# A two-layer diffusion trunk on one core: merge gates in a ring, the gated sums spread over all PSUM banks, and the modulation in other buffers

## The chip, the cores and the metric

One core of a Trainium2 chip runs the whole program in one launch. The metric is device time in microseconds (us), the median of the runs; lower is better. A profiled execution of the same kernel gives the rows that are read below.

## What is computed

The reference is one step of a two-layer trunk for 128 context tokens and 256 latent tokens (together T = 384 columns), with a model width of 1024. Cut to what matters here, a layer is

```python
mod   = silu(c) @ w_ada + b_ada                    # six vectors of 1024 for each of two token groups
h     = rmsnorm(x) * (1 + scale1) + shift1
y[n]  = branch n of h, 256 wide                    # retention, S5, gated linear, neighbourhood attention
merge = sum over n of sigmoid(h @ w_merge[n] + b_merge[n]) * (y[n] @ w_branch[n])
x     = x + gain1 * rmsnorm(merge @ w_out)
x     = x + gain2 * rmsnorm(relu(h2 @ w_mlp1)**2 @ w_mlp2)
```

All of it is in fp32. A product of two fp32 matrices is made of three matmuls of fp32r halves: high by high, low by high and high by low.

## The kernel before

Activations lie with the model width on the 128 partitions, as 8 tiles of 128 x 384, each as a high and a low half. Weights come as blocks of 128 x 1024 (512 KB) in one fixed order, written down in `weights`. The queue of the SP engine loads a block into `wf` (three buffers), the ScalarE engine (ACT) copies its high half to `wh`, the VectorE engine (DVE) subtracts to get the low half `wl` (three buffers each), and TensorE (PE) uses both. `gemm_a` multiplies one block with all 8 tiles: 24 matmuls into one PSUM bank. `next_w` hands out the next pair of halves, and moves each of the background jobs on by one piece. A job is a generator; `thin(job, 5, 4)` lets it move on in four of five such calls.

The compiler front end lays the instructions out by priority and by its own estimate of time, and puts a wait wherever an instruction needs a buffer that another still holds. On the chip every engine, and the SP queue, then takes its instructions in that fixed order. `first()` raises the priority of what is emitted under it; a job started with `PR_BG` is put 150 places back.

PSUM has eight banks, in three rings: `mm` (3), `mx` (3) and `my` (2).

The merge has 8 output tiles. For each, four gates (n = 0 to 3) are needed: `gates` makes them with four `gemm_a` into `mm`, and ACT takes each bank out with a tanh (L1415). `up` makes the four branch products of one output tile, 24 matmuls with the 6 of one branch in one bank of `mm`; DVE multiplies each bank with its gate (L1430) into `c1` (four buffers), GpSimd (POOL) adds two pairs (L1432, L1433), DVE adds the two sums (L1434), and `split` writes the high half with ACT (L121) and the low half with DVE (L122). `mixers` emits the branches' work and the first 16 gates, two rows of eight (`gt0` in `rC`, `gt1` in `rB`). `merge` then emits up 0, 1, eight gates, up 2, 3, eight gates, up 4, 5, 6, 7. After that `out_proj` loads x again (L1484, into `rX`, where the low halves of the branches were) and adds up rows of `w_out` in six banks (`acc`).

The modulation of a later part of the layer is worked out beside that. `silu_c` prepares two broadcast rows in `fa` and `fb`; for each of 24 blocks `ada` loads a block of `w_ada` (L602, into `r3`, two buffers) and runs two DVE products with a sum over the row (L604), each with its unused result in `mid` (three buffers). This job starts after the first four gates. `fb` also holds the queries, the output and the values of the neighbourhood attention, so `silu_c` cannot fill it before `put_branches` has split that output. `mid` serves the S5 output job too (`mk`, `w`, the GLU weights), and `r3` the retention job.

Of the kernel before, what the change touches and what calls it, by code (L numbers as in the profile page):

```python
# [15 lines left out]
AF = mybir.ActivationFunctionType  # L16
# [27 lines left out]
LAG0 = 2  # L44
ADA_MIX, ADA_MLP, S5_MLP = (5, 4), (2, 1), (4, 1)
NA_RATE = 2
# [8 lines left out]
class Kernel:  # L55
# [193 lines left out]
    def acc(self):  # L249

        b = [self.mmps(512), self.mmps(512), self.mmps(512), self.xps(), self.yps(), self.yps()]
        return b[0:2], b[2:4], b[4:6]

# [147 lines left out]
    def s5_setup(self):  # L401
# [6 lines left out]
        lre, lim, ldt = prm[:, 0], prm[:, 1], prm[:, 2]  # L408
        self.s5_x0 = prm[:, 3:5]
        dt, xr, xi, e = (self.sm(sh) for _ in range(4))  # L410
# [169 lines left out]
    def silu_c(self):  # L580

        nc = self.nc
        self.cb = [self.tile("fa", [128, D]), self.tile("fb", [128, 1536])[:, 0:D]]
        for g in range(2):
            cb, th = self.cb[g], self.mid([128, D])
            nc.sync.dma_start(cb, self.d["c2"][g:g + 1, :].to_broadcast([128, D]))
            nc.scalar.activation(th, cb, AF.Tanh, scale=0.5)
            nc.vector.scalar_tensor_tensor(cb, th, 1.0, cb, op0=ADD, op1=MUL)
# [6 lines left out]

    def ada(self, l, cm, first, count):

        nc = self.nc
        cols, mod = cm
        for n in range(first, first + count):  # L600
            w = self.r3([128, D])
            nc.sync.dma_start(w, self.d["w_ada"][l, n])  # L602
            for g in range(2):
                nc.vector.scalar_tensor_tensor(self.mid([128, D]), w, 0.5, self.cb[g], op0=MUL, op1=MUL,  # L604
                                               accum_out=mod[:, n, g:g + 1])
            yield
        fs = slice(first, first + count)
        b = cols[:, C_BADA + first:C_BADA + first + count].unsqueeze(2).to_broadcast([128, count, 2])
        nc.vector.tensor_tensor(mod[:, fs], mod[:, fs], b, op=ADD)
# [12 lines left out]
    def ada_first(self, xt):  # L622
# [4 lines left out]
        self.cols, self.mod = cols, mod = self.cm[0]  # L627
        fb = self.tile("fb", [128, 1536])
        cs, sel = fb[:, 0:256].rearrange("p (k m) -> p k m", k=8), fb[:, 256:260]
# [11 lines left out]
        for t in range(1, KT):  # L641
            if t == 2:
                self.s5prm = self.load("s5prm", "s5_prm", [128, 5, 16 * DEPTH], eng=nc.sync)
                with self.background(PR_SET):
                    self.s5_setup()
            if t == RAW4:
                raw = self.mid([128, 1024])
                nc.sync.dma_start(raw, self.stream.pop(0))
                self.raws.append(raw)
            ws.append(self.ada_load(t))  # L650
# [237 lines left out]
    def head_norm(self, o, gate, gn):  # L888
# [3 lines left out]
        for i in range(2):  # L892
# [5 lines left out]
            for j in range(3):  # L898
                nc.tensor.matmul(vps[:, i * 6 + 2 * j:i * 6 + 2 * j + 2], sq[:, j * 128:(j + 1) * 128], self.bones,
                                 start=True, stop=True)  # L900
        r = self.few(12)
        nc.vector.tensor_scalar(r, vps[:, 0:12], EPS, None, op0=ADD)
# [430 lines left out]
    def na_in(self, l, hs, first):  # L1333
        nc = self.nc
        self.ft = self.row("rE", shape=(128, 3072))
        self.nk = self.tile("fa", [128, 2, 512])
        fb = self.tile("fb", [128, 1536])
        self.nq = fb[:, 0:768].rearrange("p (a n) -> p a n", a=2)
        self.nv = fb[:, 768:1536].rearrange("p (a n) -> p a n", a=3)
        nc.gpsimd.dma_start(self.nk[:, :, T:512], self.d["na_k"][l])  # L1340
# [62 lines left out]

    def gates(self, tag, j, hs, within=None):

        nc = self.nc
        gt = self.row(tag)
        for e in range(2):
            if e and within:
                within()  # L1410
            for n in range(4):
                ps = self.mmps()
                self.gemm_a(ps, hs)
                c = n * 8 + 2 * j + e
                nc.scalar.activation(gt[:, e * 4 + n], ps, AF.Tanh, scale=0.5, bias=self.bmrg_h[:, c:c + 1])  # L1415
        return gt

    def up(self, dt, gt, mgh, mgl):

        nc = self.nc  # L1420
        wh, wl = self.next_w(jobs=False)
        us = []
        for n in range(4):
            ps = self.mmps()
            for k in range(2):
                ws = slice((2 * n + k) * 128, (2 * n + k + 1) * 128)
                self.mm3(ps, wh[:, ws], wl[:, ws], self.brh[:, 2 * n + k], self.brl[:, 2 * n + k], k == 0, k == 1)
            u = self.c1()
            with self.first():
                nc.vector.scalar_tensor_tensor(u, gt[:, (dt % 2) * 4 + n], 1.0, ps, op0=ADD, op1=MUL)  # L1430
            us.append(u)
        nc.gpsimd.tensor_tensor(us[0], us[0], us[1], op=ADD)  # L1432
        nc.gpsimd.tensor_tensor(us[2], us[2], us[3], op=ADD)  # L1433
        nc.vector.tensor_tensor(us[0], us[0], us[2], op=ADD)  # L1434
        self.split(mgh[:, dt], mgl[:, dt], us[0])

    def mixers(self, l, hs, hook, first):
# [18 lines left out]
        s5 = self.start(self.s5_out(l))  # L1456
        gt0 = self.gates("rC", 0, hs, lambda: hook("gates"))
        self.finish(s5)
        gt1 = self.gates("rB", 1, hs)
        self.finish(gla, ret)  # L1460
        self.put_branches()
        return gt0, gt1

    def merge(self, hs, gt0, gt1):

        mgh, mgl = self.row("rA", F32R), self.row("rD", F32R)
        self.up(0, gt0, mgh, mgl)
        self.up(1, gt0, mgh, mgl)
        gt2 = self.gates("rC", 2, hs)
        self.up(2, gt1, mgh, mgl)  # L1470
        self.up(3, gt1, mgh, mgl)
        gt3 = self.gates("rB", 3, hs)
        self.up(4, gt2, mgh, mgl)
        self.up(5, gt2, mgh, mgl)
        self.up(6, gt3, mgh, mgl)
        self.up(7, gt3, mgh, mgl)
        return [(mgh[:, k], mgl[:, k]) for k in range(KT)]
# [59 lines left out]
    def layer(self, l, hs, hook, first):  # L1537
# [6 lines left out]
        if l:  # L1544
            for i in range(3):
                nc.gpsimd.dma_start(d["x_mid"][i], self.x[:, i])
        gt0, gt1 = self.mixers(l, hs, hook, first)
        mg = self.merge(hs, gt0, gt1)
        hs, first = self.out_proj(l, mg)
# [8 lines left out]
    def weights(self, l):  # L1558
# [4 lines left out]
        br = [d["w_branch"][l, i] for i in range(8)]  # L1563
        out += mrg[0:16] + br[0:2] + mrg[16:24] + br[2:4] + mrg[24:32] + br[4:8]
        out += [d["w_out"][l, i] for i in range(8)]
# [7 lines left out]
    def run(self):  # L1573
# [11 lines left out]
        for l in range(DEPTH):  # L1585

            def hook(where):
# [7 lines left out]
                if where == "gates":  # L1595
                    self.silu_c()
                    job = chain(self.ada(l, cm[l], 16, 8), self.ada(l, cm[l], 24, 16))
                    self.start(self.thin(job, *ADA_MIX), 1, PR_BG)
                if where == "norm3" and l == 0:
                    job = chain(self.ada(0, cm[0], 40, 8), self.ada(1, cm[1], 0, 16))  # L1600
                    self.start(self.thin(job, *ADA_MLP), 1, PR_BG)
# [3 lines left out]
                if where == "norm3" and l:  # L1605
                    self.start(self.thin(self.ada(l, cm[l], 40, 8), *ADA_MLP), 1, PR_BG)

# [192 lines left out]
```

## Time and profile before

| | us |
|---|---|
| median of 3 runs | 1474.38 |
| the runs | 1471.38 to 1475.14 |
| the profiled execution, its own time | 1479.85 |
| its span, first to last instruction | 1478.1 |
| PE busy in the span | 1404.9 |
| DVE busy in the span | 933.3 |

The profiled execution is 5.5 us (0.4%) above the median. Busy time of PE counts matmuls that overlap each other, so the idle time of PE and the rate at which matmuls start say more than its busy share. In layer 0 the branches' last work and the first 16 gates run from about 222 to 320 us, the merge from 320 to 440 us and the output projection's rows after it; in layer 1 the merge runs from 1039 to 1158 us. The profile has 24 `w_ada` blocks in each layer's part of this.

### The profile page before, as it was taken

How to read it: one execution, taken by the hardware profiler on the slowest of the kernel's cores; microseconds unless marked ns; L12 is line 12 of the kernel's file. 1: busy time of each engine (PE TensorE's matmuls, PEld its weight loads, DVE VectorE, ACT ScalarE, POOL GpSimd, SP SyncE). 2: the span in 40 equal slices, each digit the busy share in tenths (PEclk: the TensorE clock that was granted, in tenths of full speed). 3: DMA queues.
4: the chain of work that ended last, by engine and by line, in shares of the span. 5: the costliest groups of instructions: out<-in, count | busy, mean ns of one | idle time of the engine just before them, and what ended most of it. 6: DMA issues, size and time to landing. Idle time of an engine off the chain costs nothing. (4 is left out here: it accounts for less than half of the span.)

```text
span 1478.1 us, 22360 instructions
## 1 busy us (share of the span) xinstructions
PE 1404.9 (95%) x8492; PEld 1246.4 (84%) x8492; DVE 933.3 (63%) x1480; ACT 664.7 (45%) x1235; POOL 352.8 (24%) x654
## 2 busy tenths in 40 slices
PE   6989989988998999999999999999799999999998
PEld 5868868878996888888989888689799789999896
DVE  4497952799565767776363397359974658333334
ACT  3446454523335544444464646544233355444443
POOL 5973790011120213320011691000110200000000
PEclk9999999999999999999999999999899999999999
DMA  9546323576434465666446423146663527433342
GB/s 379 156 128 209 113 93 101 169 236 228 134 120 166 164 197 186 198 225 199 153 139 204 142 94 111 51 154 220 210 192 125 195 73 227 135 129 126 128 152 86
DMA packets 93629, 238.17 MB, mean 161 GB/s; under 512 B 17969, under 2 KB 39505, under 8 KB 93521
## 3 DMA queue, kind: packets, MB, share of 16 engines
q1 hardware_dynamic: 90656, 227.75, 47.2%
q0 software_dynamic: 2864, 8.98, 1.9%
q8 instruction: 67, 1.10, 0.3%
q14 instruction: 42, 0.34, 0.1%
HBM read 221.72 MB, written 14.97 MB: 160 GB/s over the span
## 5 line engine op out<-in xcount | busy, mean ns | idle before, releaser
L155 DVE TENSOR_TENSOR wl<-wf,wh 128x1024 fp32r<-128x1024 f32 (+1 forms) x254 | 320.3, 1263 | 294.0 <-ACT wh L143 291.7
L143 ACT CAST wh<-wf 128x1024 fp32r<-128x1024 f32 (+1 forms) x254 | 264.5, 1045 | 453.4 <-PE mm L209 169.7
L208 PE MATMUL mm<-hh,wh 128*128 128x384 f32 (+1 forms) x712 | 246.4, 346 | 5.4 <-DVE c L1430 4.1
L210 PE MATMUL mm<-hh,wl 128*128 128x384 f32 (+1 forms) x712 | 245.0, 344 | 0.0
L209 PE MATMUL mm<-hl,wh 128*128 128x384 f32 (+1 forms) x712 | 244.4, 343 | 0.0
L208 PE MATMUL mx<-hh,wh 128*128 128x384 f32 x448 | 151.1, 337 | 0.0
L210 PE MATMUL mx<-hh,wl 128*128 128x384 f32 x448 | 150.5, 336 | 0.0
L209 PE MATMUL mx<-hl,wh 128*128 128x384 f32 x448 | 150.4, 336 | 0.0
L208 PEld LDWEIGHTS mm<-hh,wh 128*128 128x128 f32 (+1 forms) x712 | 134.6, 189 | 12.1 <-DVE c L1430 4.1
L209 PEld LDWEIGHTS mm<-hl,wh 128*128 128x128 f32 (+1 forms) x712 | 134.7, 189 | 6.3 <-issue 4.2
L210 PEld LDWEIGHTS mm<-hh,wl 128*128 128x128 f32 (+1 forms) x712 | 134.5, 189 | 5.9 <-issue 4.0
L604 DVE SCALAR_TENSOR_TENSOR mid<-r,fa 128x1024 f32<-128x1024 f32 x80 | 101.1, 1264 | 30.7 <-DMA r<-w_ada 20.5
L604 DVE SCALAR_TENSOR_TENSOR mid<-r,fb 128x1024 f32<-128x1024 f32 x80 | 100.2, 1253 | 0.2
L209 PE MATMUL mm<-wl,rA 128*128 128x512 f32 x216 | 86.8, 402 | 0.0
L208 PEld LDWEIGHTS mx<-hh,wh 128*128 128x128 f32 x448 | 84.2, 188 | 2.8 <-issue 1.0
L209 PEld LDWEIGHTS mx<-hl,wh 128*128 128x128 f32 x448 | 84.2, 188 | 1.8
L210 PEld LDWEIGHTS mx<-hh,wl 128*128 128x128 f32 x448 | 84.2, 188 | 0.2
L208 PE MATMUL mm<-wh,rA 128*128 128x512 f32 x216 | 80.2, 403 | 0.7 <-ACT rA L121 0.7
L210 PE MATMUL mm<-wh,rB 128*128 128x512 f32 x180 | 70.3, 392 | 0.0
L706 POOL TENSOR_TENSOR few<-few,negh 128x1 f32<-128x1 f32 x24 | 13.3, 553 | 220.5 <-DVE few L705 213.6
L721 POOL DMA_DIRECT2D gain<-g x4 | 2.2, 553 | 245.8 <-ACT g L720 245.8
L121 ACT CAST rA<-c 128x384 fp32r<-128x384 f32 x80 | 41.0, 513 | 44.1 <-DVE c L1434 42.3
(523 smaller groups left out, 2984.6 us busy)
## 6 DMA issues: line engine op xcount, KB each, us to landing
wf<-w_mlp SPq DMA_DIRECT2D x128, 512.0 KB, 3.4
r<-w_ada SPq DMA_DIRECT2D x82, 512.0 KB, 3.9
wf<-w_merge SPq DMA_DIRECT2D x64, 512.0 KB, 3.4
wf<-w_in SPq DMA_DIRECT2D x43, 512.0 KB, 3.9
wf<-w_branch SPq DMA_DIRECT2D x16, 512.0 KB, 3.8
wf<-w_out SPq DMA_DIRECT2D x16, 512.0 KB, 3.3
s_vt<-mid SPq DMA_DIRECT2D x16, 256.0 KB, 3.0
mid<-s_vt SPq DMA_DIRECT2D x8, 512.0 KB, 4.6
```

The lines of the kernel that those rows point to most:

```text
L121: self.nc.scalar.copy(hi, src)
L143: self.nc.scalar.copy(wh[:, :cols], raw)
L155: self.nc.vector.tensor_tensor(wl[:, :cols], raw, wh[:, :cols].bitcast(F32), op=SUB)
L208: mm(out, lh, rh, start=start, stop=False)
L209: mm(out, lh, rl, start=False, stop=False)
L210: mm(out, ll, rh, start=False, stop=stop)
L604: nc.vector.scalar_tensor_tensor(self.mid([128, D]), w, 0.5, self.cb[g], op0=MUL, op1=MUL, accum_out=mod[:, n, g:g + 1])
L706: self.nc.gpsimd.tensor_tensor(r, v, self.negh[:, 0:1], op=ALU.pow)
L721: nc.gpsimd.dma_start(d[l, which].rearrange("g (k f) -> (g k) f", f=128), rows)
```

## The change

It does four things.

- `merge` emits up(t) and then the four gates of tile t + 4, for t = 0 to 3, and then up 4 to 7. A gate tile goes to the place in `rC` or `rB` that up(t) has just read, so the two rows are a ring of four tiles. The `w_branch` blocks are moved to match in `weights`.
- `up` takes its four banks from all three rings: `my`, `my`, `mm`, `mx` for an even tile and `mx`, `mx`, `mm`, `mm` for an odd one. `acc` asks for the same six banks in another order.
- `ada` gets its buffer as an argument: within the gates and the merge the `w_ada` blocks go to `mid`, in the later part to `r3` as before. The second product writes over the block itself, and only the first uses another `mid`.
- `fb` is split into `fq` (queries and output of the attention) and `fv` (its values). `silu_c` uses `fa` and `fv`. The job starts before the first gate, and at three pieces of four calls. To make room, the S5 parameters lie in `rs`, with a small copy `s5x0` made on POOL, and a small tile of `head_norm` moves from `few` to `sm`.

```diff
-ADA_MIX, ADA_MLP, S5_MLP = (5, 4), (2, 1), (4, 1)
+ADA_MIX, ADA_MLP, S5_MLP = (4, 3), (2, 1), (4, 1)
...
     def acc(self):
-        b = [self.mmps(512), self.mmps(512), self.mmps(512), self.xps(), self.yps(), self.yps()]
-        return b[0:2], b[2:4], b[4:6]
+        b = [[self.yps(), self.yps()], [self.mmps(512), self.xps()], [self.mmps(512), self.mmps(512)]]
+        return b[::-1]
...
-        self.s5_x0 = prm[:, 3:5]
+        self.s5_x0 = self.tile("s5x0", [128, 2, n])
+        v.tensor_copy(self.s5_x0, prm[:, 3:5])
...
-        self.cb = [self.tile("fa", [128, D]), self.tile("fb", [128, 1536])[:, 0:D]]
+        self.cb = [self.tile("fa", [128, D]), self.tile("fv", [128, D])]
...
-    def ada(self, l, cm, first, count):
+    def ada(self, l, cm, first, count, buf):
...
-            w = self.r3([128, D])
+            w = buf([128, D])
             nc.sync.dma_start(w, self.d["w_ada"][l, n])
             for g in range(2):
-                nc.vector.scalar_tensor_tensor(self.mid([128, D]), w, 0.5, self.cb[g], op0=MUL, op1=MUL,
+                nc.vector.scalar_tensor_tensor(w if g else self.mid([128, D]), w, 0.5, self.cb[g], op0=MUL, op1=MUL,
                                                accum_out=mod[:, n, g:g + 1])
...
-        fb = self.tile("fb", [128, 1536])
-        self.nq = fb[:, 0:768].rearrange("p (a n) -> p a n", a=2)
-        self.nv = fb[:, 768:1536].rearrange("p (a n) -> p a n", a=3)
+        self.nq = self.tile("fq", [128, 768]).rearrange("p (a n) -> p a n", a=2)
+        self.nv = self.tile("fv", [128, D])[:, 0:768].rearrange("p (a n) -> p a n", a=3)
...
+    def gates(self, gt, t, hs):
+
+        nc = self.nc
+        for n in range(4):
+            ps = self.mmps()
+            self.gemm_a(ps, hs)
+            c = n * 8 + t
+            nc.scalar.activation(self.gate(gt, t)[:, n], ps, AF.Tanh, scale=0.5, bias=self.bmrg_h[:, c:c + 1])
+
+    def gate(self, gt, t):
+        return gt[t // 2 % 2][:, t % 2 * 4:t % 2 * 4 + 4]
...
+        banks = (self.xps, self.xps, self.mmps, self.mmps) if dt % 2 else (self.yps, self.yps, self.mmps, self.xps)
         for n in range(4):
-            ps = self.mmps()
+            ps = banks[n]()[:, 0:T]
...
-                nc.vector.scalar_tensor_tensor(u, gt[:, (dt % 2) * 4 + n], 1.0, ps, op0=ADD, op1=MUL)
+                nc.vector.scalar_tensor_tensor(u, self.gate(gt, dt)[:, n], 1.0, ps, op0=ADD, op1=MUL)
...
-        gt0 = self.gates("rC", 0, hs, lambda: hook("gates"))
+        gt = [self.row("rC")]
+        hook("gates")
+        self.gates(gt, 0, hs)
+        self.gates(gt, 1, hs)
         self.finish(s5)
-        gt1 = self.gates("rB", 1, hs)
+        gt.append(self.row("rB"))
+        self.gates(gt, 2, hs)
+        self.gates(gt, 3, hs)
...
-        self.up(0, gt0, mgh, mgl)
-        self.up(1, gt0, mgh, mgl)
-        gt2 = self.gates("rC", 2, hs)
-        self.up(2, gt1, mgh, mgl)
-        self.up(3, gt1, mgh, mgl)
-        gt3 = self.gates("rB", 3, hs)
-        self.up(4, gt2, mgh, mgl)
-        self.up(5, gt2, mgh, mgl)
-        self.up(6, gt3, mgh, mgl)
-        self.up(7, gt3, mgh, mgl)
+        for t in range(KT):
+            self.up(t, gt, mgh, mgl)
+            if t + 4 < KT:
+                self.gates(gt, t + 4, hs)
...
-        out += mrg[0:16] + br[0:2] + mrg[16:24] + br[2:4] + mrg[24:32] + br[4:8]
+        out += mrg[0:16]
+        for t in range(4):
+            out += [br[t]] + mrg[16 + 4 * t:20 + 4 * t]
+        out += br[4:8]
...
-                    job = chain(self.ada(l, cm[l], 16, 8), self.ada(l, cm[l], 24, 16))
+                    job = chain(self.ada(l, cm[l], 16, 8, self.mid), self.ada(l, cm[l], 24, 16, self.mid))
```

## Rows read from the trace of the kernel before

**Rows 1.** Waits of PE, whole span: for whom, total us, times, longest.

```profile
PE mm L208 <- DVE c L1430: 17.0, 12, 4.4
...
PE mm L208 <- ACT rC L143: 6.4, 2, 3.7
...
PE mm L209 <- DVE rX L122: 1.4, 2, 0.8
```

**Rows 2.** Windows: length, then busy us (instructions) of PE, PEld, DVE, ACT, POOL; granted clock, DMA share, GB/s.

```profile
222.00:281.00 59.00, 59.00 (x374) 50.56 (x371) 27.35 (x46) 26.69 (x55) 4.01 (x4) 1.00 0.43 123
281.00:320.00 39.00, 39.00 (x227) 35.53 (x227) 35.81 (x60) 15.58 (x25) 2.29 (x1) 1.00 0.67 216
320.00:372.00 52.00, 41.85 (x221) 39.21 (x220) 51.71 (x80) 14.32 (x21) 6.69 (x5) 0.93 0.68 223
372.00:418.00 46.00, 45.79 (x265) 45.47 (x264) 21.61 (x26) 16.70 (x22) 4.91 (x4) 1.00 0.40 129
...
1039.00:1090.00 51.00, 43.35 (x220) 41.63 (x219) 50.49 (x77) 13.99 (x19) 6.64 (x5) 0.90 0.70 225
```

**Rows 3.** The same windows, DVE's instructions of line 604 alone (read-outs counted too).

```profile
281.00:320.00 39.00, 24.09 (x41) 1.00 0.67 216
320.00:372.00 52.00, 35.42 (x56) 0.93 0.68 223
```

**Rows 4.** PE's timeline, layer 0: start, us, what; in brackets idle before, and for whom.

```profile
320.44 0.61 PE L208 MATMUL mm<-rE,wh 128*128 128x384 f32 x2
...
330.29 0.69 PE L208 MATMUL mm<-rE,wh 128*128 128x384 f32 x1 [4.42 <-DVE c L1430]
...
429.10 0.61 PE L208 MATMUL my<-wh,rA 128*128 128x512 f32 x2
...
439.52 0.39 PE L208 MATMUL mm<-wh,rA 128*128 128x512 f32 x1
440.21 0.40 PE L208 MATMUL mm<-wh,rA 128*128 128x512 f32 x1
```

**Rows 5.** PE's timeline, layer 1: the merge's first matmul and the first after it.

```profile
1039.39 0.34 PE L208 MATMUL mm<-rE,wh 128*128 128x384 f32 x1
...
1157.92 0.39 PE L208 MATMUL mm<-wh,rA 128*128 128x512 f32 x1
```

**Rows 6.** DVE's timeline in the merge of layer 0.

```profile
325.11 1.22 DVE L604 SCALAR_TENSOR_TENSOR mid<-r,fb 128x1024 f32<-128x1024 f32 x1
...
329.68 1.48 DVE L1430 SCALAR_TENSOR_TENSOR c<-rC,mm 128x384 f32<-128x384 f32 x3
...
341.89 2.03 DVE L604 SCALAR_TENSOR_TENSOR mid<-r,fa 128x1024 f32<-128x1024 f32 x1
...
350.63 1.21 DVE L155 TENSOR_TENSOR wl<-wf,wh 128x1024 fp32r<-128x1024 f32 x1
...
352.92 0.55 DVE L1434 TENSOR_TENSOR c<-c,c 128x384 f32<-128x384 f32 x1
```

**Rows 7.** Timelines of ACT and of the SP queue: the preparation for the modulation, layer 0.

```profile
247.12 1.06 ACT L587 ACTIVATE mid<-fa 128x1024 f32<-128x1024 f32 x1 [4.12 <-PE my L1016]
...
271.12 0.33 SPq L586 DMA_DIRECT2D fb<-c  x1
```

**Rows 8.** Timelines of SP, ACT and PE after the merge, layer 0.

```profile
439.54 1.87 SPq L1484 DMA_DIRECT2D rX<-x  x3
...
452.00 1.04 ACT L143 CAST rC<-wf 128x1024 fp32r<-128x1024 f32 x1 [6.57 <-DMA wf<-w_out]
...
455.38 0.63 PE L208 MATMUL mm<-rC,rA 128*128 128x512 f32 x1
...
456.66 0.63 PE L208 MATMUL mm<-wh,rA 128*128 128x512 f32 x1
```

**Rows 9.** Waits of the SP queue: for whom, total us, times, longest.

```profile
SPq L602 <- DVE mid L604: 146.6, 65, 4.1
SPq L1007 <- PE my L1020: 40.4, 2, 22.2
```

More of the change, by code (lines that the diff above doesn't have):

```diff
@@ L627, in ada_first @@
         self.cols, self.mod = cols, mod = self.cm[0]
-        fb = self.tile("fb", [128, 1536])
+        fb = self.tile("fv", [128, D])
         cs, sel = fb[:, 0:256].rearrange("p (k m) -> p k m", k=8), fb[:, 256:260]
@@ L642, in ada_first @@
             if t == 2:
-                self.s5prm = self.load("s5prm", "s5_prm", [128, 5, 16 * DEPTH], eng=nc.sync)
+                self.s5prm = self.tile("rs", [128, 768])[:, 0:80 * DEPTH].rearrange("p (a n) -> p a n", a=5)
+                nc.sync.dma_start(self.s5prm, self.d["s5_prm"])
                 with self.background(PR_SET):
@@ L900, in head_norm @@
                                  start=True, stop=True)
-        r = self.few(12)
+        r = self.sm([128, 12])
         nc.vector.tensor_scalar(r, vps[:, 0:12], EPS, None, op0=ADD)
@@ L1336, in na_in @@
         self.nk = self.tile("fa", [128, 2, 512])
-        fb = self.tile("fb", [128, 1536])
-        self.nq = fb[:, 0:768].rearrange("p (a n) -> p a n", a=2)
-        self.nv = fb[:, 768:1536].rearrange("p (a n) -> p a n", a=3)
+        self.nq = self.tile("fq", [128, 768]).rearrange("p (a n) -> p a n", a=2)
+        self.nv = self.tile("fv", [128, D])[:, 0:768].rearrange("p (a n) -> p a n", a=3)
         nc.gpsimd.dma_start(self.nk[:, :, T:512], self.d["na_k"][l])
@@ L1401, in na_mix @@
         self.out[3] = q
-    def gates(self, tag, j, hs, within=None):
+    def gates(self, gt, t, hs):
         nc = self.nc
[L1407 to L1411, printed above, removed]
-                ps = self.mmps()
[L1413 to L1416, printed above, removed]
+        for n in range(4):
[5 more added lines that the diff above has]
+        return gt[t // 2 % 2][:, t % 2 * 4:t % 2 * 4 + 4]
     def up(self, dt, gt, mgh, mgl):
@@ L1422, in up @@
         us = []
+        banks = (self.xps, self.xps, self.mmps, self.mmps) if dt % 2 else (self.yps, self.yps, self.mmps, self.xps)
         for n in range(4):
-            ps = self.mmps()
+            ps = banks[n]()[:, 0:T]
             for k in range(2):
@@ L1456, in mixers, with merge @@
         s5 = self.start(self.s5_out(l))
-        gt0 = self.gates("rC", 0, hs, lambda: hook("gates"))
+        gt = [self.row("rC")]
+        hook("gates")
+        self.gates(gt, 0, hs)
+        self.gates(gt, 1, hs)
         self.finish(s5)
-        gt1 = self.gates("rB", 1, hs)
+        gt.append(self.row("rB"))
+        self.gates(gt, 2, hs)
+        self.gates(gt, 3, hs)
         self.finish(gla, ret)
         self.put_branches()
-        return gt0, gt1
-    def merge(self, hs, gt0, gt1):
+        return gt
+    def merge(self, hs, gt):
         mgh, mgl = self.row("rA", F32R), self.row("rD", F32R)
-        self.up(0, gt0, mgh, mgl)
-        self.up(1, gt0, mgh, mgl)
-        gt2 = self.gates("rC", 2, hs)
-        self.up(2, gt1, mgh, mgl)
-        self.up(3, gt1, mgh, mgl)
-        gt3 = self.gates("rB", 3, hs)
-        self.up(4, gt2, mgh, mgl)
-        self.up(5, gt2, mgh, mgl)
-        self.up(6, gt3, mgh, mgl)
-        self.up(7, gt3, mgh, mgl)
+        for t in range(KT):
+            self.up(t, gt, mgh, mgl)
+            if t + 4 < KT:
+                self.gates(gt, t + 4, hs)
         return [(mgh[:, k], mgl[:, k]) for k in range(KT)]
@@ L1546, in layer @@
                 nc.gpsimd.dma_start(d["x_mid"][i], self.x[:, i])
-        gt0, gt1 = self.mixers(l, hs, hook, first)
-        mg = self.merge(hs, gt0, gt1)
+        gt = self.mixers(l, hs, hook, first)
+        mg = self.merge(hs, gt)
         hs, first = self.out_proj(l, mg)
@@ L1596, in hook @@
                     self.silu_c()
-                    job = chain(self.ada(l, cm[l], 16, 8), self.ada(l, cm[l], 24, 16))
+                    job = chain(self.ada(l, cm[l], 16, 8, self.mid), self.ada(l, cm[l], 24, 16, self.mid))
                     self.start(self.thin(job, *ADA_MIX), 1, PR_BG)
                 if where == "norm3" and l == 0:
-                    job = chain(self.ada(0, cm[0], 40, 8), self.ada(1, cm[1], 0, 16))
+                    job = chain(self.ada(0, cm[0], 40, 8, self.r3), self.ada(1, cm[1], 0, 16, self.r3))
                     self.start(self.thin(job, *ADA_MLP), 1, PR_BG)
@@ L1605, in hook @@
                 if where == "norm3" and l:
-                    self.start(self.thin(self.ada(l, cm[l], 40, 8), *ADA_MLP), 1, PR_BG)
+                    self.start(self.thin(self.ada(l, cm[l], 40, 8, self.r3), *ADA_MLP), 1, PR_BG)
             hs, first = self.layer(l, hs, hook, first)
```

## The prediction

> **What bounds the kernel now.** I read the waits of PE first: the engine with the most work should have few, and each has a name. Two names are near the change: PE waiting for the gated sums' DVE product, 12 times and 17.0 us, and for a weight cast at the end of the merge, 6.4 us [rows 1]. Then the windows by stage. While the first 16 gates run (222 to 320 us) PE is busy all the time; in the merge's first 52 us it is busy 41.9, at a granted clock of 0.93, and in the 46 us after that it loses 0.2 [rows 2]. Its count shows the size better: 265 matmuls in those 46 us are 0.174 us each, 221 in the 52 us are not enough to fill 39. In the bad window DVE has no room: 51.7 of 52 us, of which 35.4 are the modulation's products; in the next it works 21.6 of 46 [rows 2, 3]. Layer 1 has the same two neighbours [rows 2]. Last the timelines, for the order inside. At 320.4 PE starts the first gated sum; it stops for 4.42 us before 330.29, as the first three banks are emptied only at 329.7, behind a queue of modulation products on DVE [rows 4, 6]. So the local bound is DVE, and the three `mm` banks are how its delay reaches PE.
>
> **What the merge loses.** It holds 8 sums and 16 gates, 24 groups of 24 matmuls. At 0.174 us that is 100.0 us. Between the last sums PE also puts rows of the output projection, first at 429.10; its timeline has six such row halves before 439.52, three products each, and 18 products at 0.23 us (three between 439.52 and 440.21) are 4.2 us. So 104.2 us of work; it took 439.5 - 320.4 = 119.1 us, and 118.5 in layer 1 [rows 4, 5]. Lost: 14.9 and 14.3, **29.2 us** in both, the idle time and the slow clock after it together.
>
> **The change, part by part.**
>
> Ring order. Nothing is added: 24 groups of 24 in both. After each of the first four sums PE has four gates, 16.7 us, in which DVE can end that sum. A gate's tanh now waits for the product that reads its old place, and behind it on ACT wait the weight casts, and so PE. The first tanh falls due one gate (4.2 us) after the sum's last matmul, and its product some 3 us before that; so about 7 us of slack against a queue on DVE of at most 4.6 us now (325.1 to 329.7) [rows 6]. I cost it at nothing; without the cover it would be one cast and one gate, some 4 us, each of 8 times.
>
> DVE's load. A round of one sum and four gates is 20.9 us of PE. DVE has four products of about 0.5 (three take 1.48), the added pair and the low half of about 0.55 each, five weight halves of 1.21, and three blocks of modulation at 2 x 1.22: 2.0 + 1.1 + 6.1 + 7.3 = 16.5 us [rows 6]. Where POOL's two additions run beside it a DVE product takes 2.03 instead of 1.22 [rows 6]; two of those make 18.1. So DVE stays under PE, at 87%, where now it is at 99%.
>
> Where the modulation goes. Now it cannot start before `fb` is loaded, at 271.1, since the attention's output lies there; all 24 blocks (97 rows with the read-outs) then fall between 281 and 372 [rows 3, 7]. With `fv` that wait is gone, and the next in line is `mid`: the S5 output job holds it, and the preparation, which needs one, runs at 247.1 as soon as PE is done with it [rows 7]. I expect the first block at about 250. With three pieces in four calls, 16 calls give 12 blocks among the first gates and 16 more give 12 in the merge. In the gates' time DVE has 27.4 + 35.8 - 24.1 = 39.1 us of other work in 98; with 12 blocks, 29 us, it is at 70% [rows 2, 3]. That it is denser after 250 than before does no harm by the trace: between 281 and 320 it was 35.8 of 39, and PE lost nothing [rows 2].
>
> The banks. Eight instead of three for the sums let PE run two whole sums ahead of DVE. At the end four sums follow each other, 16.7 us of PE, against some 4.3 to 5.1 us of DVE each (four products, pair, low half, one weight half, and POOL's share): DVE falls back 1 to 4 us, which the banks hold. I cost this at nothing, or 1 us a layer where the last two banks are late for the row sums.
>
> What stays. PE's wait for the last branch's low half, 1.4 us in layer 0 [rows 1], is there whatever the order, as that branch ends with the last gates. So 29.2 - 1.4 = 27.8; I take **27**.
>
> The end of the merge. Loading x waits for the last sum, as it goes where the branches' low halves were: it is issued at 439.5, right after PE's last use. The next `w_out` blocks are issued behind it on SP, and the first is cast at 452.0, after a wait of 6.6 us; PE stood still for 3.7 us, and 2.7 in layer 1, and then ran four groups of three products at half the clock (1.28 us from 455.38 to 456.66, against 0.69 before), 2.3 us more [rows 1, 4, 8]. When the sums no longer wait for banks, the row products between them (4.2 us) come after them, so the loads are issued 4.2 us earlier against PE's work, more than the wait. At most that gives 3.7 + 2.7 + 2 x 2.3 = 11.0 us, at least nothing (if the scheduler still mixes rows in, or the row banks come late). The order of the banks speaks for the upper half, as a row bank is free only after the sixth sum: I take **7**.
>
> Small things. One copy of 64 columns on POOL in the setup, far from the end, and the in-place write: no further DVE or DMA work. S5's parameters, the small tile and the attention's two tiles change addresses only. Nothing taken, 1 us either way.
>
> **Sum.** 27 + 7 = 34 us. Against the profiled execution: 1479.9 - 34 = 1445.9. That execution is 5.5 us above the median, and none of the rows used says where, so I put the same saving on the median: 1474.4 - 34 = **1440**.
>
> **A rule beside it.** The rows say that the banks alone would not cure it, as DVE, which empties them, has 0.3 us left in 52 [rows 2]. The Trainium skill says otherwise, on its page "Perfetto Trace Analysis", section "Optimization Strategy": a gap that repeats on the engine that should be full can mean that PSUM has too few tiles. By that rule the 29 us come back even where the modulation stays bunched; by the rows only about half would. The change does both things, so the sum is the same, and only the first rival hangs on it.
>
> **The rivals.**
>
> *The modulation stays bunched.* It starts late, as `mid` is held until 247 and each block takes two of its three buffers, so that most of it still falls into the merge. For: the holder of `mid` [rows 7]. Against: 98 us of gates have room for 12 blocks [rows 2]. Then eight banks save about half of the merge's loss and little at the end: 1474 - 15 = 1459, between 1450 and 1464.
>
> *The load queue stands (slower).* SP takes its DMAs in order. Today it stands for 22.2 and 18.2 us before the S5 job's second load into `mid` [rows 9], and PE loses nothing, since six weight blocks are ahead, 6 x 4.2 = 25 us. Now `w_ada` blocks use `mid` too, and an issue that waits for it has the gates' weights behind it. The point from which it decides is a stand of 25 us; to eat up the 34 us it would take 17 us more in each layer, so 42 us. At 50 us it costs 25 in each layer, 1474 - 34 + 50 = 1490. For: twice the users of one ring. Against: the longest wait of a `w_ada` issue for its buffer's reader is 4.1 us in 65 [rows 9], and these loads have the lower priority. The Trainium skill, on its page "DMA: Bandwidth & Descriptors", section "Anatomy of one DMA — SWDGE (gpsimd) path", states that a DMA's semaphore wait happens on the issuing sequencer before dispatch; that is the same mechanism, and the trace agrees, with the 22.2 us.
>
> *The gain does not arrive.* What PE waits for in the merge is taken by another wait of the same size, of the tanh for its ring place or of a weight half behind modulation products. For: DVE at 87%. Against: the 7 us of slack. Time: within 4 us of 1474.
>
> **How the numbers follow.** The forecast has 0.58, with 1431 to 1449 (all of both terms, 1474.4 - 29.2 - 11 - 3 for the spread of the runs, to four fifths of the first alone, with 2 for the small things). The first rival has 0.26, the gain that does not arrive 0.09, the slower one 0.07. A measurement of this kernel tells about 0.3%, 4.4 us, from no change: faster is 0.58 + 0.26 = 0.84, same 0.09, slower 0.07. The range takes in the forecast and most of the first rival: 1431 to 1462.
>
> **What would show it.** PE's waits for the gated sums' product fall from 17 us to under 4; the merge takes about 100 us plus the row products, at full clock; the modulation's products begin near 250 and end near 405 in layer 0, and no window of DVE is full; x is loaded right after the last sum and PE's wait for the `w_out` cast is under 2 us. It is wrong if DVE is still full for 30 us from the merge's start, if PE waits for weights among the first gates, or if the row sums wait for their banks.

## The result, and the profile after

The kernel with the change takes 1455.87 us (1453.53 to 1458.91, 4 runs) where the kernel before takes 1473.93 beside it: ratio 0.9881, 95% interval 0.9854 to 0.9908, so 18 us faster. The forecast was 1440 and the range 1431 to 1462: the sign and the range held, but the saving is about half of the 34 us that the sum gave. Its profiled execution has a span of 1451.8 us against 1478.1. The boundary is the step behind a merge's row sums, with the residual and the next norm; PE's first product behind it (L291) marks the same work in both kernels, and so does PE's first product of layer 1. Cut at these marks, the spans compare as follows (us; "again" is a second profiled execution of each kernel, on other chips).

| stretch | before | after | before, again | after, again |
|---|---|---|---|---|
| start to the boundary of layer 0 | 478.8 | 460.8 | 481.9 | 464.9 |
| from there to layer 1's input | 291.0 | 292.3 | 291.0 | 291.6 |
| layer 1's input to its boundary | 426.2 | 416.2 | 422.7 | 417.8 |
| from there to the end | 282.1 | 282.5 | 282.1 | 282.5 |
| of these: first gated sum to boundary, layer 0 | 158.4 | 143.1 | 158.9 | 144.3 |
| first gated sum to boundary, layer 1 | 156.6 | 144.6 | 155.5 | 144.9 |
| layer 1's input to its first gated sum | 269.6 | 271.6 | 267.2 | 272.9 |

So the merges with their ends give back 27.3 us in the first pair and 25.2 in the second, and layer 1 ahead of its merge loses 2.0 and 5.7 of it again. Layer 0 ahead of its first gated sum is 2.7 and 2.5 shorter.

PE's waits after, whole span (for whom, total us, times, longest):

```profile
PE mx L901 <- DVE g L899: 4.5, 1, 4.5
PE mm L208 <- ACT rC L143: 4.2, 2, 2.3
PE mx L533 <- DVE c L574: 4.0, 1, 4.0
...
PE mx L208 <- ACT wh L143: 2.6, 2, 1.6
```

The 17.0 us for the gated sums' product [rows 1] are gone from the list altogether. A new wait of 4.5 us stands near the top: PE waits in layer 1 for a DVE copy of `head_norm` (L899). The wait of 4.0 us (L574) lies at 103 us, in the early part of layer 0; the kernel before has 0.8 there. The windows of the merges after, same columns as [rows 2], and below them DVE's modulation products alone (L605 now), as in [rows 3]:

```profile
320.00:372.00 52.00, 51.01 (x290) 50.21 (x290) 50.85 (x75) 18.94 (x25) 9.57 (x6) 1.00 0.66 214
372.00:418.00 46.00, 46.00 (x266) 46.00 (x265) 27.43 (x38) 16.77 (x22) 8.14 (x7) 1.00 0.41 137
1025.00:1077.00 52.00, 50.40 (x288) 49.86 (x287) 50.40 (x77) 17.32 (x23) 6.03 (x5) 1.00 0.67 221
```

```profile
250.00:281.00 31.00, 10.86 (x17) 1.00 0.70 216
281.00:320.00 39.00, 21.37 (x37) 1.00 0.66 207
320.00:372.00 52.00, 27.09 (x43) 1.00 0.66 214
```

In its first 52 us the merge now runs 290 matmuls at full granted clock, where 221 ran at 0.93 [rows 2]. The modulation did move forward: 10.86 us of it lie ahead of 281 us, none did before, and 27.09 instead of 35.42 fall into the merge. But DVE is still nearly full there, 50.85 of 52 (the prediction's round had it at 87%), and PE hardly notices. The end of the merge, SP, ACT and PE after:

```profile
420.04 1.37 SPq L1483 DMA_DIRECT2D rX<-x  x3
425.75 0.33 SPq L164 DMA_DIRECT2D wf<-w_out  x1
...
436.08 1.04 ACT L143 CAST rC<-wf 128x1024 fp32r<-128x1024 f32 x1 [4.39 <-DMA wf<-w_out]
...
437.18 0.51 PE L208 MATMUL mm<-rC,rA 128*128 128x512 f32 x1 [2.28 <-ACT rC L143]
```

x is loaded right behind the last sum, 19.5 us earlier than in [rows 8]; the late cast of `w_out` still stops PE for 2.28 us (3.7 before).

### The profile page after: what moved, and what is told of

The parts are those of the page before. It is cut to its first block, busy times and chain, and to the rows that moved or that the text cites. A ratio compares the mean times of both kernels' runs of the same rounds, so it can differ in the third digit from the quotient of the medians.

```text
span 1451.8 us, 22299 instructions
## 1 busy us (share of the span) xinstructions
PE 1394.5 (96%) x8492; PEld 1241.7 (86%) x8492; DVE 934.8 (64%) x1480; ACT 663.5 (46%) x1235; POOL 350.7 (24%) x655
## 5 line engine op out<-in xcount | busy, mean ns | idle before, releaser
L143 ACT CAST wh<-wf 128x1024 fp32r<-128x1024 f32 (+1 forms) x254 | 264.6, 1045 | 415.6 <-PE mx L209 170.8
L605 DVE SCALAR_TENSOR_TENSOR mid<-mid,fa 128x1024 f32<-128x1024 f32 x48 | 60.4, 1259 | 27.0 <-DMA mid<-w_ada 26.8
L605 DVE SCALAR_TENSOR_TENSOR mid<-mid,fv 128x1024 f32<-128x1024 f32 x48 | 60.0, 1250 | 0.2
L1432 POOL TENSOR_TENSOR c<-c,c 128x384 f32<-128x384 f32 x16 | 17.5, 1091 | 174.6 <-DVE c L1430 111.2
```

The lines of the kernel that those rows point to most:

```text
L143: self.nc.scalar.copy(wh[:, :cols], raw)
L605: nc.vector.scalar_tensor_tensor(w if g else self.mid([128, D]), w, 0.5, self.cb[g], op0=MUL, op1=MUL, accum_out=mod[:, n, g:g + 1])
```

## The experiments

### The parts one by one

The change has three parts: the **ring** (order of sums, gates and their weights), the **banks** (the sums' PSUM banks and the order of the row banks), and the **modulation** (buffers `fv`, `fq`, `mid`, and the start ahead of the gates). All combinations ran. The table gives the median, its ratio to the kernel before on the same chip, and PE's longest kinds of wait in the merges. In every run that has it, the modulation part includes its early start.

| run | ring | banks | modulation | us | ratio, 95% interval | PE waits in the merges (both layers) |
|---|---|---|---|---|---|---|
| e1 | - | - | - | 1478.46 | 1.0007, 0.9982 to 1.0031 | product 15.6 |
| e2 | - | - | yes | 1480.45 | 1.0008, 0.9981 to 1.0036 | product 8.2, last branch's split 7.3 |
| e4 | - | yes | - | 1476.80 | 0.9981, 0.9958 to 1.0005 | product 21.2 |
| e9 | yes | - | - | 1468.47 | 0.9911, 0.9878 to 0.9944 | product 12.6 |
| e3 | yes | yes | - | 1448.05 | 0.9790, 0.9761 to 0.9818 | none for either |
| e6 | yes | - | yes | 1480.74 | 1.0025, 1.0010 to 1.0039 | split 9.9, product 7.2 |
| e7 | - | yes | yes | 1478.77 | 1.0019, 1.0000 to 1.0039 | product 16.1 |
| e5 | yes | yes | yes | 1458.12 | 0.9876, 0.9854 to 0.9897 | product 0.4 |

Where the time goes in the profiles (us, from PE's timelines, cut as above):

| run | first gated sum to boundary, layer 0 and 1 | layer 1's input to its first gated sum |
|---|---|---|
| e1 (none) | 158.9, 155.5 | 267.2 |
| e2 (modulation) | 152.7, 151.6 | 280.2 |
| e4 (banks) | 159.1, 155.9 | 264.6 |
| e9 (ring) | 156.9, 148.3 | 267.4 |
| e3 (ring, banks) | 143.1, 146.1 | 264.2 |
| e6 (ring, modulation) | 150.6, 149.6 | 282.3 |
| e7 (banks, modulation) | 154.4, 155.0 | 273.4 |
| e5 (all) | 144.3, 144.9 | 272.9 |

In layer 1 of e3 and e4, 22 products of a gate (some 3.8 us) run behind the first gated sum that stand ahead of it in the others. In e2 and e6 the wait for the last branch's split comes just ahead of the first gated sum (4.6 and 7.0 us in layer 1), so it counts in the last column.

**e1, the kernel before again**, no edit.

> The kernel before, unchanged, profiled once more. If its first profiled execution was simply a slow one, the new span lies near 1472 us, and the merges (first gated sum to the load of x) take some 113 to 117 us each instead of 119.1 and 118.6. If a profile always shows it slow, the span is again 1477 to 1480 with merges of 118 to 120. The median stays within 0.3% of 1474.

1478.46 us, and its profile has merges of 119.6 and 117.7 us from first sum to the load of x, against 119.1 and 118.6: the profiled execution that the prediction read was typical of the merges.

**e2, the modulation alone.** The kernel before with its new buffers, three pieces in four, and the start ahead of the gates:

```diff
-        gt0 = self.gates("rC", 0, hs, lambda: hook("gates"))
+        hook("gates")
+        gt0 = self.gates("rC", 0, hs)
```

> The modulation's part alone (fv, fq, mid for the blocks, start before the first gate, three in four); the order of sums and gates and the three banks stay as before. If DVE's bunched modulation is the cause, most of the gain is here: 1460 to 1465, PE's waits for the gated sums' product fall from 17 to under 8 us, and DVE in the merge's first 52 us from 51.7 to about 40. If the banks are the cause, 1469 to 1474 with these waits still over 10 us.

```profile
320.00:372.00 52.00, 46.49 (x245) 45.26 (x246) 46.38 (x72) 15.81 (x23) 6.70 (x5) 0.93 0.62 200
```

```profile
PE mm L208 <- DVE c L1431: 8.2, 8, 2.8
PE mm L208 <- ACT rE L121: 7.3, 2, 4.6
```

Nothing is gained in all: ratio 1.0008. In layer 0 the stretch to the boundary is 7.6 us shorter than in e1 (474.3 against 481.9), in layer 1 it is 9.2 longer (431.9 against 422.7). DVE is at 46.38 of 52 us in the first merge, not at the 40 that were expected, and PE's waits for the product fall from 15.6 to 8.2 us. From the first gated sum to the boundary the two layers are 10.0 us shorter than in e1; but 7.3 us of a new wait, for the last branch's split, stand just ahead of that sum, and layer 1 has the 4.5 us wait for `head_norm` as well. So most of what the freer DVE brings behind the first sum is given back just ahead of it, and the wait for `head_norm` comes on top. What the move would be worth in the old order without its early start was not tried.

**e3, ring and banks, the modulation as before** (after the first four gates, in `fb` and `r`):

```diff
-        hook("gates")
         self.gates(gt, 0, hs)
+        hook("gates")
         self.gates(gt, 1, hs)
```

> Ring order and banks without the modulation's part: its blocks still start after fb is loaded, near 281 us, and crowd DVE until about 370. If the bunched modulation is the cause: 1463 to 1470, and PE waits for something else of DVE (low halves of the weights) in the merge's first 50 us. If order and banks are what counts: 1455 to 1460, as with the whole change, and no PE wait over 1 us in the merge although DVE is full.

The fastest of the eight, 1448.05 us. Its windows in the two merges (columns as in [rows 2]):

```profile
320.00:372.00 52.00, 50.77 (x291) 50.14 (x290) 52.00 (x79) 18.89 (x25) 5.85 (x4) 1.00 0.75 243
1020.00:1072.00 52.00, 52.00 (x301) 52.00 (x300) 51.36 (x78) 19.62 (x26) 6.09 (x5) 1.00 0.76 248
```

DVE is busy 52.00 of 52 us, 30.99 of them with the modulation's products, fuller than in the kernel before (51.71), and PE works 50.77 and 52.00. It is faster than both expectations. With this order and these banks a full DVE does not hold the merge.

**e4, the banks alone:**

```diff
-            ps = self.mmps()
+            ps = banks[n]()[:, 0:T]
```

> Only the eight banks for the sums (and the matching order in acc); two sums in a row and then eight gates, modulation as before. If three banks are how DVE's delay reaches PE, and nothing else, it gives nearly all: 1456 to 1462. If DVE, being full, passes the delay on another way (gates whose place the sums must have read first, weight halves): 1466 to 1472.

```profile
PE mm L208 <- DVE c L1431: 21.2, 3, 10.1
```

Neither expectation came in, and the wait for the product did not shrink; it moved. PE now runs the two sums that stand together without a stop, and the gates behind them, which still use the `mm` banks, wait up to 10.1 us for a product. The Trainium skill says on its page "Perfetto Trace Analysis", section "Optimization Strategy", that a gap which repeats on the engine that should be full can mean too little room in PSUM. Here more banks alone changed the time by 0.2%, within the interval.

**e9, the ring alone**, run later, with the banks and the modulation of the kernel before:

```diff
-        out += mrg[0:16] + br[0:2] + mrg[16:24] + br[2:4] + mrg[24:32] + br[4:8]
+        out += mrg[0:16]
+        for t in range(4):
+            out += [br[t]] + mrg[16 + 4 * t:20 + 4 * t]
+        out += br[4:8]
```

> Only the ring order of the merge and of its weights; the sums keep the three mm banks and the modulation its place after the first four gates. Theory A (the order gives PE something to do while DVE is late, but only banks of their own let PE go past a sum that is stuck, so each alone is worth nothing and the two together 2.1%): within 0.4% of before, 1471 to 1482 us, PE still waiting over 10 us in the merges for the sums' products or for the last branch's low half. Theory B (the order carries the gain, and the loss of modulation with ring was made by the modulation part): 1455 or less, PE's waits in the merges under 5 us.

```profile
320.00:372.00 52.00, 43.89 (x218) 42.08 (x217) 51.98 (x81) 14.75 (x21) 7.24 (x5) 0.87 0.70 224
1040.00:1092.00 52.00, 46.96 (x265) 45.40 (x264) 52.00 (x79) 16.34 (x21) 7.99 (x6) 1.00 0.71 232
```

Neither expectation: 0.9% faster. Layer 1's merge has 265 matmuls in 52 us instead of 220 in 51 [rows 2], layer 0's has no more than before. So the order carries some of the gain by itself, and only with the banks the whole of it: ring 0.9%, banks 0.2%, both 2.1%. With DVE equally full in e9 and e3, what the banks add is that PE can go on to a gate while a sum stands unfinished.

**e5, the kernel after again**, no edit.

> The changed kernel once more, for its spread and for the base of the runs beside it: median 1453 to 1459; merges of 102 to 103 us in every profile if they are set by the schedule, and the spread of the runs (1453.5 to 1458.9 so far) then comes from elsewhere.

1458.12 us, ratio 0.9876; the merges take 102.7 and 103.2 us from the first sum to the load of x, as expected.

**e6, ring and modulation**, the kernel after with the old banks:

```diff
-            ps = banks[n]()[:, 0:T]
+            ps = self.mmps()
```

> The change without its banks: modulation early, ring order, sums in the three mm banks. If room on DVE is what counts: within 3 us of the whole change, 1455 to 1459, PE's waits for the gated sums' product under 3 us except in the four last sums. If the banks count by themselves: 1463 or more, waits over 8 us.

```profile
PE mm L208 <- ACT rE L121: 9.9, 2, 7.0
...
PE mm L208 <- DVE c L1429: 7.2, 6, 2.8
```

Slower than before by 0.25%, and 1.1% slower than the ring alone. PE waits up to 7.0 us for the split of a late branch, just ahead of layer 1's first gated sum, which comes 15.1 us later after the layer's input than in e1. In e3 and in the kernel after PE's timeline has the first sum's parts in `mm` and `mx`, then a gate, and the parts in `my` after it; with three banks taken in turn the parts follow each other, and PE stands.

**e7, banks and modulation**, the kernel after without the ring:

```diff
-        for t in range(KT):
-            self.up(t, gt, mgh, mgl)
-            if t + 4 < KT:
-                self.gates(gt, t + 4, hs)
+        self.up(0, gt0, mgh, mgl)
+        self.up(1, gt0, mgh, mgl)
+        gt2 = self.gates("rC", 2, hs)
...
```

> The change without its ring: modulation early, eight banks, two sums in a row and then eight gates, and the first modulation calls earlier. If the ring only spreads DVE's work, which now has room, this is the same as the whole change, 1454 to 1459. If the order itself counts: 1460 or more.

1.0019: the two parts that the prediction thought decisive for DVE's queue, together, without the ring, gain nothing. The merges are 5.0 us shorter than in e1, and layer 1 ahead of its merge is 6.2 longer.

### What the modulation costs

With the ring the modulation part costs time: e3 to e5 is 0.9790 to 0.9876, e9 to e6 0.9911 to 1.0025. The new wait says where to look. SP and PE in layer 1, kernel after again (e5):

```profile
923.85 0.33 SPq L587 DMA_DIRECT2D fa<-c  x1
931.05 0.33 SPq L587 DMA_DIRECT2D fv<-c  x1
931.43 4.10 SPq L1009 DMA_DIRECT2D mid<-s_strip  x8
...
936.58 1.44 PE L901 MATMUL mx<-bones,c 128*128 128x2 f32 x6 [4.49 <-DVE g L899]
```

The silu's second load into `fv` waits for the attention's last reader, and the S5 output job's loads of `s_strip` stand behind it on SP. In e3 they are issued at 797.26. (In layer 0 they move as well, from 147 us in the kernel before to 221 in the kernel after.) The reading to be tested: late, they leave PE with nothing but the norm's chain, and ACT makes the S5 job's 12 copies just ahead of that norm's square (L898). Two kernels test this.

**e10, the kernel after with the start behind the first four gates**, buffers as after:

```diff
         gt = [self.row("rC")]
-        hook("gates")
         self.gates(gt, 0, hs)
+        hook("gates")
         self.gates(gt, 1, hs)
```

> The kernel after, but the silu of the condition and the modulation's job begin behind the first four gates, as before; the new buffers stay. Theory A (the modulation part costs 9 us because the early silu goes ahead of the S5 output job on SP and in the mid ring, and that job's loads come 110 us later in layer 1): 1446 to 1451 us, PE waits for head_norm's copy (4.5 us) gone, layer 1 from its input to the boundary some 6 us shorter than in the kernel after. Theory B (the buffers cost it, as the w_ada blocks share the mid ring): 1455 to 1459 us, no change.

```profile
793.73 2.03 SPq L1009 DMA_DIRECT2D mid<-s_strip  x3
...
930.42 0.33 SPq L587 DMA_DIRECT2D fv<-c  x1
```

The norm's square on ACT, e5 and then e10; in e10 it runs ahead of the 12 copies, and the 4.5 us wait is gone:

```profile
935.45 0.49 ACT L898 ACTIVATE c<-mx 128x384 f32<-128x384 f32 x1
```

```profile
929.84 0.49 ACT L898 ACTIVATE c<-mx 128x384 f32<-128x384 f32 x1 [2.02 <-PE mx L896]
```

1450.28 us, ratio 0.9798 (0.9757 to 0.9838): the buffers cost nothing, the early start costs what separates e3 from the kernel after. And it buys nothing for its price: in e10 the silu's second load goes out at 930.42, in e5 at 931.05, and e10 has 12.29 us of the modulation's products between 250 and 281 us, the kernel after 10.86. What differs is what stands around the silu in the fixed order of the queues. The window 900 to 950 us of layer 1, e5 and then e10:

```profile
900.00:950.00 50.00, 43.46 (x250) 33.81 (x249) 18.37 (x35) 25.30 (x68) 1.66 (x3) 0.90 0.35 102
```

```profile
900.00:950.00 50.00, 46.73 (x275) 35.66 (x274) 17.62 (x37) 26.41 (x72) 3.38 (x3) 0.93 0.27 86
```

Busy time times granted clock is 39.1 us in e5 and 43.5 in e10: 4.4 us more work in the same time. Layer 1 from its input to its boundary is 5.7 us shorter in e10 (412.1 against 417.8); at its first gated sum 3.0 of them are there, and 2.7 come behind it. In layer 0 e10's boundary comes at 460.8: 4.1 earlier than in e5, but no earlier than in the first profile of the kernel after. The 4.0 us wait at 103 us is gone in e10 too, but e6 and e7, which start early, don't have it either. That part stays open.

**e11, the S5 output job's first loads put out ahead of the silu**, the early start kept:

```diff
         gt = [self.row("rC")]
+        next(s5)
         hook("gates")
```

> The kernel after, but the first piece of the S5 output job (its loads of s_strip and s_w) is put out ahead of the silu; the modulation still begins ahead of the first gates. Theory A (it is the place of these loads behind the silu's second load on SP): s_strip of layer 1 is issued near 800 us again instead of 927, PE's wait of 4.5 us for head_norm's copy is gone, 1447 to 1453 us. Theory B (it is the early modulation products on DVE, or the mid ring shared with w_ada): 1455 to 1459 us, the wait remains or moves into the first gates.

`s_strip` is issued at 803.99 and the 4.5 us wait is gone, as expected; but the time is 1474.29 us (0.9964, 0.9939 to 0.9989), 16 us worse than the kernel after and outside both expectations. The loss is in the merges, 151.7 and 153.5 us from first sum to boundary instead of 144.3 and 144.9 in e5; some 2 us of that in each layer are 30 small products of `head_norm` that run ahead of the first sum in e5 and behind it here. PE, DVE and the window of layer 0:

```profile
332.96 0.62 PE L208 MATMUL my<-rE,wh 128*128 128x384 f32 x2 [1.38 <-ACT rE L121]
...
336.55 0.69 PE L209 MATMUL my<-rX,wh 128*128 128x384 f32 x1 [2.09 <-DVE rX L122]
```

```profile
331.23 0.61 DVE L914 SCALAR_TENSOR_TENSOR rD<-rD,rgh 128x384 f32<-128x384 f32 x1
331.76 1.22 DVE L605 SCALAR_TENSOR_TENSOR mid<-mid,fv 128x1024 f32<-128x1024 f32 x1
332.90 0.08 DVE L605 DVE_READ_ACCUMULATOR mid<-mid,fv 128x1 f32 x1
332.90 0.61 DVE L914 SCALAR_TENSOR_TENSOR rD<-rD,rgh 128x384 f32<-128x384 f32 x1
```

```profile
320.00:372.00 52.00, 47.72 (x272) 46.15 (x272) 47.88 (x75) 16.22 (x23) 9.13 (x5) 0.93 0.61 196
```

In this kernel the last branch's closing products (L914) run on DVE at 331.2 and 332.9, with a modulation product between them, 13 and 14 us after the first gated sum (318.5); in the kernel after they begin at 320.7, 3 us after it. PE catches up with that branch, stands idle for 4.3 us of the window and has a clock of 0.93 in it. In e10 PE has no wait for this branch. So the S5 loads' place makes the 4.5 us wait, but putting it right does not give the time back: one load put right brought out another wait. That the early start disturbs the whole order in which the last branches come due fits these rows, but no run shows it by itself; how much of the price is the S5 loads' stays open.

### The end of the merge

**e8, x loaded after the last `w_out` block**, else the kernel after: the three issues of `rX<-x` move behind the last `w_out` issue on SP.

```diff
-        for i in range(3):
-            nc.sync.dma_start(self.x[:, i], d["x"][i] if l == 0 else d["x_mid"][i])
+        self.late_x = [d["x"][i] if l == 0 else d["x_mid"][i] for i in range(3)]
```

> The changed kernel, but the three loads of x are issued after the last w_out block instead of before it (x is first needed some 20 us later). If the end of the merge is held by x's 1.5 MB ahead of the last w_out blocks on the queue: PE's wait for the cast into rC (2.3 and 2.0 us in after) goes, the half clock after it too, and the time falls by 5 to 9 us. If it is held by the late cast of the third w_out block behind DVE's sums (issue 5.7 us after x's in after), the loads land little earlier and it falls by 0 to 3 us. A loss is possible if the residual then waits for x.

1459.89 us, ratio 0.9886 (0.9866 to 0.9906), no different from e5. PE's waits for that cast are still 3.4 us in all (4.2 in the kernel after). x ahead of the weights is not what keeps most of the wait.

**e12, three additions left out in each of the last two sums:**

```diff
-        nc.gpsimd.tensor_tensor(us[0], us[0], us[1], op=ADD)
-        nc.gpsimd.tensor_tensor(us[2], us[2], us[3], op=ADD)
-        nc.vector.tensor_tensor(us[0], us[0], us[2], op=ADD)
+        if dt < 6:
+            nc.gpsimd.tensor_tensor(us[0], us[0], us[1], op=ADD)
+            nc.gpsimd.tensor_tensor(us[2], us[2], us[3], op=ADD)
+            nc.vector.tensor_tensor(us[0], us[0], us[2], op=ADD)
```

> The kernel after; in the last two of the eight gated sums the three additions over the branches (two on POOL, one on DVE) are left out, so that the split follows the first product at once; the rest is unchanged. It asks what keeps the wait for the third late w_out cast at the end of the merge (2.3 us in layer 0, then about 2 us of half clock). Theory A (the casts of w_out stand on ACT behind the splits of the last sums, which wait for POOL's and DVE's additions, so that the weight buffers come free late): casts and the next w_out issues 2 to 3 us earlier, PE's waits for rC and rB at the end of the merges (6 us in all) under 2 us, 1448 to 1453 us. Theory B (the loads themselves take their time there, with x beside them): the issues come earlier but the waits stay within 1 us, 1454 to 1459 us.

```profile
422.06 1.37 SPq L1484 DMA_DIRECT2D rX<-x  x3
425.61 8.89 SPq L164 DMA_DIRECT2D wf<-w_out  x3
...
437.39 1.05 ACT L143 CAST rC<-wf 128x1024 fp32r<-128x1024 f32 x1 [3.55 <-DMA wf<-w_out]
```

1456.10 us, ratio 0.9847 (0.9813 to 0.9881). The first `w_out` issue comes 3.6 us after that of x instead of 5.7; but the cast of `rC` comes 15.3 us after it instead of 16.0, and PE's waits for it are 1.5 and 1.6 us instead of 2.3 and 2.0. The cast of `rC` that PE waits for takes the second of these three blocks, and that one hardly moved. Its issue in the kernel after, with the two loads of `gain` on POOL's queue just ahead:

```profile
428.88 1.11 POOL L726 DMA_DIRECT2D rB<-gain  x2 [2.29 <-DMA gain<-g]
...
429.96 0.33 SPq L164 DMA_DIRECT2D wf<-w_out  x1
```

That is 9.9 us after x; in e12 it is 9.4 (431.46 us), as SP waits before it for DVE's low half (`wl`, 4.2 and 5.4 us) to free a weight buffer. By the view of DMA issues the block then takes 6.1 and 5.9 us to land, against 3.2 for the four `w_out` blocks issued between 400 and 419 us. x is not what it shares the DMA engines with: from 428.5 to 429.9 they are at 0.05, as x has landed, and from 430 to 436, with the `gain` blocks, at 0.93. In e8 it lands in 4.3 us, but its issue, behind the same wait on DVE (5.7 us), comes later against PE's work. So e12 did not test its theory A, as the additions that it leaves out did not bring this issue forward. A late issue and a slow landing make the wait; which of them is worth more was not tried.

## Why the prediction was half right

**What bounds the kernel.** The place was right (the first 52 us of each merge), the cause only in part. The prediction read DVE at 51.7 of 52 [rows 2, 3] as the bound. e3 has DVE at 52.00 and loses 1.2 us of PE; e2, with DVE at 46.38, takes 10.0 us off the merges behind the first sums, stands 7.3 us more just ahead of them, and gains nothing in all. What the change removed was PE's order: two sums in a row, on banks shared with the gates, whose products sat in DVE's queue. DVE's delay mattered only because PE had no other work that it was allowed to begin.

**The merge, 27 us.** First sum to the load of x, less the 4.2 us of row products that stood between the sums before, goes from 114.9 to 102.3 us in layer 0 and from 114.4 to 102.9 in layer 1 (PE's timeline has 18 more of them ahead of the load of x before than after, in both layers). That is 24.1 us of 27, and 23.1 in the second pair of profiles: the size was right, but not for the reason given. DVE did not get the room that the prediction worked out, 87% of a round; it is at 50.85 of 52, and the time came back all the same. The ring's waits, costed at nothing, are indeed not seen: no tanh stops PE, and the weight casts (`wh`) cost it 2.6 us in all.

**The banks, "about half".** Wrong: 0.2% alone, within its interval. "The modulation's move", meant to do the other half, gives 1.0008 alone and 1.0019 with the banks, both with the early start's price in them. With ring and banks it is worth nothing that these runs can tell: e10, which has the move without the price, takes 1450.28 us, e3 1448.05. The ring, costed only for its risks, is the part without which nothing comes, and the banks more than double what it brings. The merge's term was saved by the change doing all of it at once; that was luck. The rule that the prediction set against its rows (the banks bring it back even where the modulation stays bunched) holds only with the ring.

**The modulation's cost, nothing.** This is the step that failed in the sum. The prediction followed the silu's buffers (`fv` for `fb`, then `mid`) and found the start near 250 us, and it is 253.6. It did not follow what was queued behind the silu's loads on SP: the S5 output job's loads, which in layer 1 had gone out more than 100 us ahead, and in layer 0 some 60. Its slower rival named this mechanism (SP in order, users of `mid`) but looked at the gates' weights behind it, not at the S5 job's loads. The price is 7.8 us by the medians of e5 and e10; by their profiles it is 9.9, 4.1 of them in layer 0 and 5.7 in layer 1.

**The end of the merge, 7 us.** Mis-sized. From the load of x to the boundary took 39.3 and 38.0 us; with the 4.2 us of row products moved behind it, that makes 43.5 and 42.2, and it is 40.8 and 41.7 now: 3.2 us in both layers. The step "issued 4.2 us earlier against PE's work, more than the wait" left out that a weight buffer comes free only behind DVE's low half: the block that PE waits for is issued 9.9 us after x. It also left out that this block takes 6.1 us to land beside those of `gain`.

**The sum.** 24.1 + 3.2 = 27.3 us came of 34; outside the merges the first pair of profiles loses 1.0 and the second 4.4 (span 1477.6 to 1456.8). The medians show 18, nearer to the second pair, whose spans differ by 20.8. The first rival's 1459 lies near the measured time, but not for its reason: the modulation did not stay bunched, and e3, where it did, is the fastest.

**What was to show it.** PE's waits for the product under 4 us: yes, none. The merge at about 100 us and full clock: yes. The products from 250: yes, but they end near 373, not 405 (1.02 us of them are left behind 372). No full window of DVE: no, 50.85 of 52, and the prediction would have called itself wrong on that. PE's wait for the cast under 2 us: no, 2.28.

## What to carry to other kernels

An engine that is full for 50 us beside a starved TensorE is not yet its bound: ask first which work TensorE could do in that time and what keeps it from starting it, the order of its instructions or the banks they share; here neither alone was worth more than 0.9%, both together 2.1%. Read a part that shows no gain stretch by stretch: e2's zero is a shorter merge and a longer way to it. Where a job is moved forward, list what is issued behind its loads on the same queue, also in the later layers, where these loads may have had 100 us of lead. The version to keep is ring and banks with the modulation started where it was, 1448.05 us (e3), or 1450.28 with the new buffers (e10), which these runs can't tell apart.

## What the runs showed of the hardware

One wait costs more than its length. After the 4.5 us wait in layer 1 of the kernel after (927.7 to 932.2 us) the first products of the next gate take 0.52 us instead of 0.34:

```profile
934.01 0.52 PE L209 MATMUL mm<-hl,wh 128*128 128x384 f32 x1
...
936.52 0.34 PE L208 MATMUL mm<-hh,wh 128*128 128x384 f32 x1
```

They follow each other by 0.32 us until 936.25 and by 0.175 from 936.52 on, the slow and the full level of the clock; the granted clock is 1.00 from 920 to 927.7 us, 0.71 in the wait, 0.51 from 932.2 to 936.5 and 1.00 again behind it. And the loads beside each other at the end of the merge: 512 KB took 6.1 us to land beside the two blocks of `gain`, with the DMA engines at 0.93, against 3.2 for the `w_out` blocks before x.
